# The experts' loop of a hybrid encoder block: weight loads in longer runs, low parts and loads on other queues, earlier gathers

## The chip, the core and the metric

The kernel runs on one core of a Trainium2 chip. Its time is the device time of one execution in microseconds (us), and less is better. The engines are named as the profile names them: PE is TensorE's matrix unit and PEld its weight load, DVE is VectorE, ACT is ScalarE, POOL is GpSimd, SP is the sync engine, which here only issues DMAs. Each engine works through its own queue in order and waits for semaphores.

## The reference, cut

The block is a bidirectional mixer (a long convolution and a state space scan) followed by a mixture of experts, each with a residual and a layer norm. 1024 tokens of 1024 values go through it, in float32. The change lies in the mixture of experts: a router picks 8 of 64 experts for each token, and each expert is a gated two-layer network with 256 hidden values.

```python
def routed_experts(h2d, idx, w, w_gate, w_up, w_down):
    ...
    def step(acc, blk):
        tok, wt, e = blk
        xb = h_pad[tok]
        hb = jax.nn.silu(xb @ w_gate[e]) * (xb @ w_up[e])
        yb = (hb @ w_down[e]) * wt[:, None]
        return acc.at[tok].add(yb.astype(acc.dtype)), None
...
def moe_sublayer(h, router_w, router_bias, exp_w_gate, exp_w_up, exp_w_down,
                 sh_w_gate, sh_w_up, sh_w_down):
    ...
    idx, w = route(h2d, router_w, router_bias)
    routed = routed_experts(h2d, idx, w, exp_w_gate, exp_w_up, exp_w_down)
    shared = (jax.nn.silu(h2d @ sh_w_gate) * (h2d @ sh_w_up)) @ sh_w_down
    return (routed + shared).reshape(bsz, seq, d)
...
    h = layer_norm(DN_ALPHA * h + ffn, ln2_g[i], ln2_b[i])
```

## The kernel before, in words

The stages before the experts (projections, scan, convolutions, merge, router) take the first 2350 us or so and are not touched, except for one view in the shared expert (`sh_gu`). The experts' loop is in `moe`.

The router sorts the experts by load, so that the place of an expert in that order (its rank r) has a fixed capacity `caps[r]`: 16 experts of 192 rows, 16 of 160, 16 of 128 and 16 of 112. `order` takes a large and a small one in turn. Each expert is cut into blocks of at most 128 rows; three blocks (128, then 64 or 32, then 128 or 112 rows) make two experts, and there are 96 blocks in all. Index tables (`slot_tables`) tell which token each row of a block holds. They are made for eight experts at a time, during the eight experts before, one step of the generator `tj` per block; each step compares on DVE (line 2071, tile oh) and multiplies on PE (line 2079).

Every float32 matmul is done as products of a high and a low part (`mm3`: three matmuls, `both_mm`: two with the parts of the rows side by side, for blocks of 32 or 64 rows). An expert's weights come as three tiles of 1 MB, numbered p: two with four k-slices each of gate and up, one with down. For each tile there are three steps. `w_load` issues the DMA into a raw buffer eraw (line 1599). `w_hi` rounds on ACT to ehi (line 1611). `w_lo` subtracts to elo (line 1618): on DVE for the two gate and up tiles, on POOL for the down tile. When the low part is done the raw buffer is free, and `lo_load` at once issues the load of tile p + 6 into it.

The gate and up slices of one k lie next to each other in a raw tile (256 values of gate, 256 of up), so that one matmul takes 512 columns of both. The source of a DMA has 4 KB in a row for each partition, but each 1 KB of it goes to another place.

For each block b the loop does, in this order: `gather(b + 3)` (POOL, an indirect DMA from h_d into a tile xg, line 1625); the casts `w_hi` of two tiles; the gate and up matmuls, with `lo_load` of a tile and `hidden(b - 1)` between k = 3 and k = 4; the activation; `xpose(b + 2)`, which transposes gathered rows on PE (line 1640) and splits them into xgh and xgl; `lo_load` of the second tile; a table step; `down(b - 1)`, the down matmuls, whose result yo (two buffers) an indirect DMA of POOL adds into scr_acc in HBM (line 1661). These scatter-adds read and write the same tensor, so each waits until the one before it has landed. `hidden` transposes the activated rows and splits them into hb (line 74). For the small blocks the activation goes through a tile lows, whose last step is the product of line 1877 on DVE.

The rows xg have three buffers: one in the pool of raw tiles, for every third block, and two elsewhere. `gather(b + 3)` writes the buffer that `xpose(b)` has read.

All five engines run in the order in which the code issues the instructions (`manual_schedule`). The loads of gate and up are on SP's queue, the down load, the gathers, the scatters and the low part of down on POOL's.

Of the kernel before, what the change touches and what calls it, by code (L numbers as in the profile page):

```python
# [9 lines left out]
F32 = mybir.dt.float32  # L10
# [5 lines left out]
ALU = mybir.AluOpType  # L16
# [3 lines left out]
P = 128  # L20
ET = mybir.EngineType
MANUAL = {ET.SP, ET.PE, ET.Activation, ET.DVE, ET.Pool}
D = 1024
# [18 lines left out]
class Kern:  # L42
# [107 lines left out]
    def w_load(self, pool, c0, n=P):  # L150
        raw = pool.tile([P, KT, P], F32, name="wraw", bufs=2)
        self.nc.sync.dma_start(raw[:, :, :n], self.a["w_in"][0, :, c0:c0 + n].rearrange("(k p) c -> p k c", p=P))
        return raw
# [1056 lines left out]
    def merge(self):  # L1210
        nc, a, tc = self.nc, self.a, self.tc
# [105 lines left out]
        with ExitStack() as cx:  # L1317
            cx.callback(p1.release)
            pool = cx.enter_context(tc.tile_pool(name="mh", bufs=1, reuse_waits="tile"))
# [16 lines left out]
            for p in range(3):  # L1336
# [4 lines left out]
                for o in range(2 if p == 0 else 0, 8):  # L1341
                    i = p * 8 + o
                    ps = [self.bank(), self.bank()]
# [12 lines left out]
                    elif p == 1:  # L1356
                        for h in range(2):
                            v = sr[o][:, h * 512:(h + 1) * 512]
                            TT(v, v, ps[h], ALU.add)
                        STT(sr[o], gt.pop((p, o)), 1.0, sr[o], ALU.add, ALU.mult)  # L1360
                    else:
                        g = gt.pop((p, o))
                        for h in range(2):
                            v = g[:, h * 512:(h + 1) * 512]
                            STT(v, v, 1.0, ps[h], ALU.add, ALU.mult)
                        TT(g, g, sr[o], ALU.add)
                        for h in range(2):
                            v = g[:, h * 512:(h + 1) * 512]
# [85 lines left out]
                    sh[q] = [[v[:, h * 512:(h + 1) * 512] for v in hl] for h in range(2)]  # L1454

            def sh_gu(t):
                gu = [sh[k // 2][k % 2] for k in range(8)]
                for k, ps in enumerate(self.swi_gu(lhs(t), gu, P)):
                    if k < 7:
                        yield  # L1460
                yield self.swi_act(pool, ps, P, ld()[:, 0:256])
# [100 lines left out]
    def moe(self):  # L1562
# [3 lines left out]
        with ExitStack() as cx:  # L1566
# [17 lines left out]
            def w_load(p):  # L1584
                if p >= 192:
                    return
                i, q = divmod(p, 3)
                eng = nc.gpsimd if q == 2 else nc.sync
                if q != 1:
                    weng[0] = eng.value_load(self.eid[0:1, order[i]:order[i] + 1], min_val=0, max_val=63)  # L1590
                g, u, d = [a[n][0][bass.ds(weng[0], 1)].rearrange("o (p j) c -> (o p) j c", p=P)
                           for n in ("exp_w_gate", "exp_w_up", "exp_w_down")]
                parts = ((g[:, 0:4], u[:, 0:4]), (g[:, 4:8], u[:, 4:8]), (d,))[q]
                wraw[p] = rps[i % 2].tile([P, 2048], F32, name="eraw", bufs=3)
                v = wraw[p].rearrange("p (k c) -> p k c", k=parts[0].shape[1])
                c0 = 0
                for src in parts:
                    n = src.shape[2]
                    eng.dma_start(v[:, :, c0:c0 + n], src)
                    c0 += n  # L1600

            def w_hi(p, c=slice(0, 2048)):
                if p >= 192:
                    return
                if p not in whl:
                    i, q = divmod(p, 3)
                    hi, lo = whl[p] = [wps[i % 2].tile([P, 2048], F32R, name=f"e{c}", bufs=3) for c in ("hi", "lo")]
                    k = 2 if q == 2 else 4
                    wsplit.setdefault(i, []).extend(zip(*[[v.rearrange("p (k c) -> p k c", k=k)[:, j] for j in range(k)]
                                                          for v in (hi, lo)]))  # L1610
                nc.scalar.copy(whl[p][0][:, c], wraw[p][:, c])  # L1611

            def w_lo(p, c=slice(0, 2048)):
                if p >= 192:
                    return
                eng = nc.gpsimd if p % 3 == 2 else nc.vector
                hi, lo = whl[p]
                eng.tensor_tensor(lo[:, c], wraw[p][:, c], hi[:, c].bitcast(F32), ALU.subtract)  # L1618

            def gather(b):  # L1620
                if b >= len(blocks):
                    return
                i, r, s, o, n = blocks[b]
                t = rps[0].tile([P, D], F32, name="xg") if b % 3 == 0 else pool.tile([P, D], F32, name="xg", bufs=2)
                nc.gpsimd.indirect_dma_start(out=t[:n, :], out_offset=None, in_=self.h_d,  # L1625
                                             in_offset=bass.IndirectOffsetOnAxis(ap=tabs[r][s][0], axis=0))
                gath[b] = t

            def xpose(b):
                if b >= len(blocks):  # L1630
                    return
                i, r, s, o, n = blocks[b]
                t = gath.pop(b)
                xh = pool.tile([P, 8, P], F32R, name="xgh", bufs=2)
                xl = xh[:, :, n:2 * n] if n in (32, 64) else pool.tile([P, 8, P], F32R, name="xgl", bufs=2)
                for h in range(2):
                    ps = self.bank("B")
                    for j in range(4):
                        k = h * 4 + j
                        nc.tensor.transpose(ps[:, j * P:j * P + n], free(t[:n, k:k + 1], [[8, P]]), self.ident[:n, :n])  # L1640
                    src = ps.rearrange("p (j t) -> p j t", t=P)[:, :, :n]
                    self.split(src, xh[:, h * 4:h * 4 + 4, :n], xl[:, h * 4:h * 4 + 4, :n])
                xts[b] = xh[:, :, :2 * n] if n in (32, 64) else [(xh[:, k, :n], xl[:, k, :n]) for k in range(8)]

            def hidden(b):
                if b >= 0:
                    n = blocks[b][4]
                    hbs[b] = (self.both_h if n in (32, 64) else self.swi_h)(pool, sgs.pop(b), n)

            def down(b):  # L1650
                if b < 0 or b >= len(blocks):
                    return
                i, r, s, o, n = blocks[b]
                y = pool.tile([P, D], F32, name="yo", bufs=2)
                wd = [[(h[:, q * 512:(q + 1) * 512], l[:, q * 512:(q + 1) * 512]) for q in range(2)] for h, l in wsplit[i][8:10]]
                if n in (32, 64):
                    self.both_down(hbs.pop(b), wd, y, n)
                else:
                    for q, ps in enumerate(p for p in self.swi_down(pool, hbs.pop(b), wd, n) if p is not None):
                        nc.scalar.activation(y[:n, q * 512:(q + 1) * 512], ps[:n, :], AF.Copy, scale=tabs[r][s][2])  # L1660
                nc.gpsimd.indirect_dma_start(  # L1661
                    out=self.acc_d, out_offset=bass.IndirectOffsetOnAxis(ap=tabs[r][s][1], axis=0),
                    in_=y[:n, :], in_offset=None, compute_op=ALU.add, oob_is_err=True, bounds_check=L + P - 1)
# [37 lines left out]
            cw.enter_context(tc.manual_schedule(engines=MANUAL))  # L1701
            gather(1)
            gather(2)
            for p in range(3, 6):
                w_load(p)
            xpose(0)
            for p in range(2):
                for c in [slice(c * 512, c * 512 + 512) for c in range(4)]:
                    w_hi(p, c)
                    w_lo(p, c)  # L1710
                w_load(p + 6)
            xpose(1)
            tj = iter(())

            def lo_load(p):
                w_lo(p)
                w_load(p + 6)
            for b, (i, r, s, o, n) in enumerate(blocks):
                if s == 0:
                    if i % 8 == 0 and i < 56:  # L1720
                        for _ in tj:
                            pass
                        tj = table_jobs(i // 8 + 2)
                gather(b + 3)
                w_hi(2 * b + 2)
                w_hi(2 * b + 3)
                x, gu = xts.pop(b), wsplit[i][0:8]
                for k, ps in enumerate((self.both_gu if n in (32, 64) else self.swi_gu)(x, gu, n)):
                    if k == 3:
                        lo_load(2 * b + 2)  # L1730
                        hidden(b - 1)
                if n in (32, 64):
                    sgs[b] = self.both_act(pool, ps, tabs[r][s][2], n)
                else:
                    sgs[b] = self.swi_act(pool, ps, n)
                xpose(b + 2)
                lo_load(2 * b + 3)
                next(tj, None)
                down(b - 1)
# [82 lines left out]

    def swi_gu(self, lhs, gu, n):
        ps = self.bank()
        for k in range(8):
            self.mm3(ps[:n, :], lhs[k][0], lhs[k][1], gu[k][0], gu[k][1], k == 0, k == 7)
            yield ps

    def swi_act(self, pool, ps, n, sg=None):
# [34 lines left out]

    def both_gu(self, x, gu, n):
        ps = self.bank()
        for k in range(8):
            self.both_mm(ps, x[:, k], n, gu[k][0], gu[k][1], k == 0, k == 7)
            yield ps

    def both_act(self, pool, ps, w, n):
# [499 lines left out]
```

## Time and profile before

| | |
|---|---|
| median of 3 runs | 3530.07 us (3528.78 to 3532.55) |
| the profiled execution | 3534.84 us, span from first to last instruction 3533.2 us |
| busy share of the span | PE 90%, DVE 73%, POOL 47%, ACT 40% |
| mean granted clock of TensorE | 0.943 of full |
| mean DMA rate | 152 GB/s |
| gate and up loads | 256 DMAs of 512 KB on SP's queue |
| down loads | 64 DMAs of 1024 KB on POOL's queue |
| gathers, scatters | 96 and 96 indirect DMAs on POOL's queue |

The profile lists one execution. An instruction's row has its start from the beginning of the span, its length, its engine and line, the tiles out<-in, and in brackets how long the engine was idle before it and what ended that. Shares of busy time are means over stages with different limits, so a stage has to be read by itself. A DMA queue's share is the time that its packets took, over 16 DMA engines.

### The profile page before, as it was taken

To read this page: it belongs to the slowest core of one execution; us is meant where nothing else is said; L and a number is where in the kernel's file an instruction comes from. 1 tells how busy PE (TensorE), PEld (TensorE's weight loads), DVE (VectorE), ACT (ScalarE), POOL (GpSimd) and SP (SyncE) were. 2 spreads that over 40 slices of the span, in tenths; PEclk is the share of its full clock that TensorE was granted. 3 is DMA by queue.
4 is the path that set the end of the run, shared out by engine and by line. 5 is a ranking of instruction groups with operands and counts; after the bars stand their busy time and mean duration, and the time that the engine had idled before them with its cause. 6 is when DMAs were issued, how large, how long until landed. Compare 5 with 4: busy or idle time off the path is not lost. (4 is left out here: it accounts for less than half of the span.)

```text
span 3533.2 us, 42386 instructions
## 1 busy us (share of the span) xinstructions
PE 3188.0 (90%) x14923; PEld 2506.6 (71%) x14923; DVE 2590.6 (73%) x3551; ACT 1406.7 (40%) x2206; POOL 1676.7 (47%) x1480
## 2 busy tenths in 40 slices
PE   8989998989998998899999999997889888888893
PEld 6767776777777777567888888875666666666662
DVE  6787887888787878557994344657778787677786
ACT  3334333343334232322223212415656555565663
POOL 2545454555454546441110320215667667777774
PEclk9999899999999999899999999988999999899996
DMA  4323232322322322744325445327999899888894
GB/s 131 78 72 87 67 96 75 85 73 79 91 78 75 89 72 91 215 147 151 106 90 173 126 155 158 107 85 242 271 271 270 259 259 262 250 249 249 250 283 128
DMA packets 439908, 538.22 MB, mean 152 GB/s; under 512 B 24361, under 2 KB 373325, under 8 KB 430989
## 3 DMA queue, kind: packets, MB, share of 16 engines
q1 hardware_dynamic: 404717, 379.23, 36.6%
q0 software_dynamic: 33824, 152.06, 15.0%
q10 hardware_dynamic: 1152, 4.19, 0.3%
q8 instruction: 119, 1.95, 0.2%
q14 instruction: 96, 0.79, 0.1%
HBM read 430.29 MB, written 105.12 MB: 152 GB/s over the span
## 5 line engine op out<-in xcount | busy, mean ns | idle before, releaser
L170 PE MATMUL bankA<-xth,whi 128*128 128x512 f32 (+1 forms) x1424 | 470.1, 412 | 0.5 <-ACT whi L73 0.3
L170 PE MATMUL bankA<-xtl,whi 128*128 128x512 f32 (+1 forms) x1424 | 452.6, 400 | 0.0
L170 PE MATMUL bankA<-xth,wlo 128*128 128x512 f32 (+1 forms) x1424 | 449.4, 397 | 1.5 <-POOL wlo L74 1.5
L1618 DVE TENSOR_TENSOR elo<-eraw,ehi 128x2048 fp32r<-128x2048 f32 (+1 forms) x134 | 393.7, 2945 | 18.9 <-ACT ehi L1611 13.1
L1661 POOL DMA_INDIRECT scr_acc<-yo,sidx x96 | 231.1, 2407 | 275.9 <-DMA scr_acc<-yo,sidx 147.1
L1611 ACT CAST ehi<-eraw 128x2048 fp32r<-128x2048 f32 (+1 forms) x198 | 356.3, 1852 | 3.3 <-DMA eraw<-in_exp_w_gate_dram 3.3
L74 POOL TENSOR_TENSOR wlo<-wraw,whi 128x1024 fp32r<-128x1024 f32 (+1 forms) x89 | 225.4, 2532 | 278.1 <-ACT whi L73 278.1
L170 PEld LDWEIGHTS bankA<-xtl,whi 128*128 128x128 f32 (+1 forms) x1424 | 274.5, 193 | 64.1 <-DVE xtl L74 0.4
L170 PEld LDWEIGHTS bankA<-xth,wlo 128*128 128x128 f32 (+1 forms) x1424 | 272.2, 191 | 64.5 <-POOL wlo L74 2.0
L170 PEld LDWEIGHTS bankA<-xth,whi 128*128 128x128 f32 (+1 forms) x1424 | 268.2, 195 | 58.3 <-issue 5.4
L1618 POOL TENSOR_TENSOR elo<-eraw,ehi 128x2048 fp32r<-128x2048 f32 x64 | 298.1, 4658 | 15.8 <-ACT ehi L1611 14.7
L399 POOL TENSOR_SCALAR Wm<-cbm,dt 128x128 f32<-128x128 f32 x256 | 129.9, 507 | 348.2 <-DVE cbm L373 348.2
L1625 POOL DMA_INDIRECT xg<-scr_h,gidx x96 | 182.3, 1899 | 63.4 <-issue 24.3
L79 PE MATMUL bankA<-elo,xgh 128*128 128x512 f32 (+1 forms) x512 | 203.6, 398 | 8.6 <-DVE elo L1618 8.6
L78 PE MATMUL bankA<-ehi,xgh 128*128 128x512 f32 (+1 forms) x512 | 210.1, 410 | 0.0
L80 PE MATMUL bankA<-ehi,xgl 128*128 128x512 f32 (+1 forms) x512 | 203.3, 397 | 0.0
L1640 PE MATMUL bankB<-ident,xg 128*128 128x128 f32 (+3 forms) x768 | 113.4, 295 | 94.0 <-DMA xg<-scr_h,gidx 92.5
L1640 PEld LDWEIGHTS bankB<-ident,xg 128*128 128x128 f32 (+3 forms) x768 | 101.5, 198 | 122.9 <-issue 107.5
L74 DVE TENSOR_TENSOR xgl<-bankB,xgh 128x512 fp32r<-128x512 f32 (+1 forms) x128 | 81.3, 664 | 107.7 <-ACT xgh L73 106.0
L80 PE MATMUL bankA<-ehi,hb 128*128 128x512 f32 (+1 forms) x256 | 121.3, 474 | 27.0 <-DVE hb L74 26.9
L1877 DVE SCALAR_TENSOR_TENSOR lows<-lows,wt 64x256 f32<-64x256 f32 (+1 forms) x32 | 132.5, 4140 | 15.5 <-ACT lows L1876 15.5
L393 DVE SCALAR_TENSOR_TENSOR Em<-bcs,Acs,Em 128x128 f32<-128x128 f32 x256 | 140.9, 609 | 2.3
(551 smaller groups left out, 7672.7 us busy)
## 6 DMA issues: line engine op xcount, KB each, us to landing
eraw<-in_exp_w_gate_dram SPq DMA_DIRECT2D x128, 512.0 KB, 5.9
eraw<-in_exp_w_down_dram POOLq DMA_DIRECT2D x64, 1024.0 KB, 6.0
eraw<-in_exp_w_up_dram SPq DMA_DIRECT2D x128, 512.0 KB
wraw<-in_w_in_dram SPq DMA_DIRECT2D x88, 512.0 KB, 4.1
bcs<-scr_at SPq DMA_DIRECT2D x128, 256.0 KB, 5.6
scr_K<-kout SPq DMA_DIRECT2D x32, 512.0 KB, 2.8
Kt<-scr_K SPq DMA_DIRECT2D x32, 512.0 KB, 3.5
scr_gate<-accf SPq DMA_DIRECT2D x16, 512.0 KB, 4.2
```

Source lines behind the costliest of these rows:

```text
L74: (lo_eng or nc.vector).tensor_tensor(lo, src, hi.bitcast(F32), ALU.subtract)
L78: mm(out, sh, mh, start=first, stop=False)
L79: mm(out, sh, ml, start=False, stop=False)
L80: mm(out, sl, mh, start=False, stop=last)
L170: mm(ps[h], wt[:, k, :n], x[:, h * 512:(h + 1) * 512], start=(k == 0 and f == 1), stop=(k == KT - 1 and l == 1))
L393: STT(E[:, h], bcs[:, 1, h], self.A[:, c, 32 + j:33 + j], E[:, h], ALU.subtract, ALU.min)
L1611: nc.scalar.copy(whl[p][0][:, c], wraw[p][:, c])
L1618: eng.tensor_tensor(lo[:, c], wraw[p][:, c], hi[:, c].bitcast(F32), ALU.subtract)
L1625: nc.gpsimd.indirect_dma_start(out=t[:n, :], out_offset=None, in_=self.h_d, in_offset=bass.IndirectOffsetOnAxis(ap=tabs[r][s][0], axis=0))
L1640: nc.tensor.transpose(ps[:, j * P:j * P + n], free(t[:n, k:k + 1], [[8, P]]), self.ident[:n, :n])
L1661: nc.gpsimd.indirect_dma_start(out=self.acc_d, out_offset=bass.IndirectOffsetOnAxis(ap=tabs[r][s][1], axis=0), in_=y[:n, :], in_offset=Non ...
L1877: nc.vector.scalar_tensor_tensor(t[:, 0:256], t[:, 0:256], w, t[:, 256:512], ALU.mult, ALU.mult)
```

## The change

The raw tiles of gate and up hold first the four slices of gate, then those of up, so that each DMA writes 4 KB in a row per partition; the matmuls take their 512 columns as two pieces of 256. Down loads are issued by SP and the low part of down is made on DVE, so POOL keeps only gathers and scatters. Raw tiles rotate over five buffers instead of six (three in one pool, two in the other), so a tile's successor is p + 5; the result tile yo has four buffers instead of two. `gather(b + 5)` behind `xpose(b + 2)` takes the place of `gather(b + 3)` at the block's start, and two more gathers stand ahead of the loop. `hidden(b - 1)` comes before the `lo_load` of k = 3. In the blocks of every eighth expert a second table step stands at k = 5. The line numbers move by up to four.

```diff
@@ sh_gu
-                gu = [sh[k // 2][k % 2] for k in range(8)]
+                gu = [[v.rearrange("p (s c) -> p s c", s=2) for v in sh[k // 2][k % 2]] for k in range(8)]
@@ w_load
-                eng = nc.gpsimd if q == 2 else nc.sync
-                if q != 1:
+                eng = nc.sync
+                if q == 0:
                     weng[0] = eng.value_load(self.eid[0:1, order[i]:order[i] + 1], min_val=0, max_val=63)
...
-                wraw[p] = rps[i % 2].tile([P, 2048], F32, name="eraw", bufs=3)
-                v = wraw[p].rearrange("p (k c) -> p k c", k=parts[0].shape[1])
-                c0 = 0
-                for src in parts:
-                    n = src.shape[2]
-                    eng.dma_start(v[:, :, c0:c0 + n], src)
-                    c0 += n
+                wraw[p] = rps[p % 5 // 3].tile([P, 2048], F32, name="eraw", bufs=3 - p % 5 // 3)
+                v = wraw[p].rearrange("p (s k c) -> p s k c", s=len(parts), k=parts[0].shape[1])
+                for n, src in enumerate(parts):
+                    eng.dma_start(v[:, n], src)
@@ w_hi
-                    k = 2 if q == 2 else 4
-                    wsplit.setdefault(i, []).extend(zip(*[[v.rearrange("p (k c) -> p k c", k=k)[:, j] for j in range(k)]
+                    k, n = (2, 1) if q == 2 else (4, 2)
+                    wsplit.setdefault(i, []).extend(zip(*[[v.rearrange("p (s k c) -> p k s c", s=n, k=k)[:, j] for j in range(k)]
@@ w_lo
-                eng = nc.gpsimd if p % 3 == 2 else nc.vector
                 hi, lo = whl[p]
-                eng.tensor_tensor(lo[:, c], wraw[p][:, c], hi[:, c].bitcast(F32), ALU.subtract)
+                nc.vector.tensor_tensor(lo[:, c], wraw[p][:, c], hi[:, c].bitcast(F32), ALU.subtract)
@@ down
-                y = pool.tile([P, D], F32, name="yo", bufs=2)
+                y = pool.tile([P, D], F32, name="yo", bufs=4)
@@ ahead of the loop
-            for p in range(3, 6):
+            for p in range(3, 5):
                 w_load(p)
             xpose(0)
+            gather(3)
...
-                w_load(p + 6)
+                w_load(p + 5)
             xpose(1)
+            gather(4)
             tj = iter(())

             def lo_load(p):
                 w_lo(p)
-                w_load(p + 6)
+                w_load(p + 5)
@@ the loop over blocks
-                gather(b + 3)
                 w_hi(2 * b + 2)
                 w_hi(2 * b + 3)
...
                     if k == 3:
+                        hidden(b - 1)
                         lo_load(2 * b + 2)
-                        hidden(b - 1)
+                    if k == 5 and i % 8 == 0:
+                        next(tj, None)
...
                 xpose(b + 2)
+                gather(b + 5)
                 lo_load(2 * b + 3)
@@ swi_gu, and both_gu alike
+        p3 = ps[:n, :].rearrange("p (s c) -> p s c", s=2)
         for k in range(8):
-            self.mm3(ps[:n, :], lhs[k][0], lhs[k][1], gu[k][0], gu[k][1], k == 0, k == 7)
+            self.mm3(p3, lhs[k][0], lhs[k][1], gu[k][0], gu[k][1], k == 0, k == 7)
```

On POOL, about halfway through the loop, three blocks (two experts) of the kernel before stand in its queue like this; TENSOR_LOAD and ISA read the expert's number for the down load.

```order
L1661 DMA scr_acc<-yo,sidx_22035 1152x1024
L1625 DMA xg<-scr_h,gidx_23292 128x1024
L1618 TENSOR_TENSOR elo<-eraw,ehi 128x2048
L1590 TENSOR_LOAD eid
L1590 ISA x2
L1599 ISA
L1599 DMA eraw<-in_exp_w_down_dram 128x2048
L1661 DMA scr_acc<-yo,sidx_22022 1152x1024
L1625 DMA xg<-scr_h,gidx_23305 32x1024
L1618 TENSOR_TENSOR elo<-eraw,ehi 128x2048
```

The same engine and place in the changed kernel:

```order
L1621 DMA xg<-scr_h,gidx_22836 32x1024
L1657 DMA scr_acc<-yo,sidx_21638 1152x1024
L1621 DMA xg<-scr_h,gidx_22823 112x1024
L1657 DMA scr_acc<-yo,sidx_21625 1152x1024
L1621 DMA xg<-scr_h,gidx_22823 128x1024
```

What moved: the low part and the down load have left this queue, and a gather now stands two blocks further ahead of the scatter beside it.

On DVE, a small block and the large one behind it, at about the same place, before:

```order
L74 TENSOR_TENSOR hb<-bankC,hb 128x256
L1875 TENSOR_TENSOR lows<-lows,bankA 64x512
L1877 SCALAR_TENSOR_TENSOR lows<-lows,wt_22037 64x256
L74 TENSOR_TENSOR xgl<-bankB,xgh 128x512 x2
L1618 TENSOR_TENSOR elo<-eraw,ehi 128x2048
L74 TENSOR_TENSOR hb<-bankC,hb 128x2x64
L1834 TENSOR_TENSOR sg<-sg,bankA 128x256
L74 TENSOR_TENSOR xgh<-bankB,xgh 128x4x32 x2
L1618 TENSOR_TENSOR elo<-eraw,ehi 128x2048
```

and now:

```order
L74 TENSOR_TENSOR hb<-bankC,hb 128x256
L1614 TENSOR_TENSOR elo<-eraw,ehi 128x2048
L1877 TENSOR_TENSOR lows<-lows,bankA 64x512
L1879 SCALAR_TENSOR_TENSOR lows<-lows,wt_21640 64x256
L74 TENSOR_TENSOR xgl<-bankB,xgh 128x512 x2
L1614 TENSOR_TENSOR elo<-eraw,ehi 128x2048
L74 TENSOR_TENSOR hb<-bankC,hb 128x2x64
L1614 TENSOR_TENSOR elo<-eraw,ehi 128x2048
L1835 TENSOR_TENSOR sg<-sg,bankA 128x256
L74 TENSOR_TENSOR xgh<-bankB,xgh 128x4x32 x2
L1614 TENSOR_TENSOR elo<-eraw,ehi 128x2048
```

What moved: each block now has two low parts, the first of them behind hb and ahead of the block's own activation.

On SP, one expert's loads before, and then now:

```order
L1599 DMA eraw<-in_exp_w_gate_dram 128x4x256
L1599 ISA
L1599 DMA eraw<-in_exp_w_up_dram 128x4x256
L1599 ISA
L1599 DMA eraw<-in_exp_w_gate_dram 128x4x256
L1599 ISA
L1599 DMA eraw<-in_exp_w_up_dram 128x4x256
```

```order
L1597 DMA eraw<-in_exp_w_gate_dram 128x1024
L1597 ISA
L1597 DMA eraw<-in_exp_w_up_dram 128x1024
L1597 ISA
L1597 DMA eraw<-in_exp_w_gate_dram 128x1024
L1597 ISA
L1597 DMA eraw<-in_exp_w_up_dram 128x1024
L1597 ISA
L1597 DMA eraw<-in_exp_w_down_dram 128x2048
```

What moved: the down load stands behind the others of its expert, and what a partition receives of a gate or up DMA is one piece of 1024 values instead of four of 256.

## Rows read from the trace of the kernel before

**Rows 1.** Windows: stretch, its length, busy time by engine, PEclk, DMA share, GB/s.

```profile
2450.00:3450.00 1000.00, 878.38 (x4397) 659.90 (x4395) 773.84 (x763) 597.30 (x747) 701.96 (x299) 0.93 0.90 261
3400.00:3450.00 50.00, 45.95 (x204) 33.14 (x204) 39.30 (x46) 32.63 (x42) 31.52 (x16) 0.97 0.97 289
```

**Rows 2.** Waits, 2450 to 3450 us: total us, times, longest us.

```profile
POOL scr_acc L1661 <- DMA scr_acc<-yo,sidx: 147.1, 32, 8.0
...
PE bankB L1640 <- DMA xg<-scr_h,gidx: 91.2, 35, 5.5
...
PE bankA L80 <- DVE hb L74: 20.4, 18, 1.9
```

**Rows 3.** Timeline of POOL: start us, length us, instruction, idle before it.

```profile
2907.61 2.47 POOL L1625 DMA_INDIRECT xg<-scr_h,gidx  x1 [0.30 <-issue]
2916.50 1.46 POOL L1661 DMA_INDIRECT scr_acc<-yo,sidx  x1 [6.41 <-DMA scr_acc<-yo,sidx]
2918.26 0.99 POOL L1625 DMA_INDIRECT xg<-scr_h,gidx  x1 [0.30 <-PE bankB L1640]
2919.27 4.60 POOL L1618 TENSOR_TENSOR elo<-eraw,ehi 128x2048 fp32r<-128x2048 f32 x1
...
2925.06 2.44 POOL L1661 DMA_INDIRECT scr_acc<-yo,sidx  x1 [0.30 <-issue]
...
2937.71 1.62 POOL L1661 DMA_INDIRECT scr_acc<-yo,sidx  x1 [3.12 <-DMA scr_acc<-yo,sidx]
...
2947.60 1.45 POOL L1661 DMA_INDIRECT scr_acc<-yo,sidx  x1 [4.96 <-DMA scr_acc<-yo,sidx]
```

**Rows 4.** Timeline of PE across a wait for a gather.

```profile
2913.38 0.40 PE L79 MATMUL bankA<-elo,xgh 128*128 128x512 f32 x1
2913.61 0.40 PE L80 MATMUL bankA<-ehi,xgl 128*128 128x512 f32 x1
2917.55 1.13 PE L1640 MATMUL bankB<-ident,xg 128*128 128x128 f32 x8 [3.54 <-DMA xg<-scr_h,gidx]
...
2919.56 0.63 PE L78 MATMUL bankA<-ehi,hb 128*128 128x512 f32 x1
2919.98 0.63 PE L79 MATMUL bankA<-elo,hb 128*128 128x512 f32 x1
```

**Rows 5.** Page part 6, a weight load: KB, median us from issue to landing.

```profile
eraw<-in_exp_w_gate_dram SPq DMA_DIRECT2D x128, 512.0 KB, 5.9
```

**Rows 6.** Groups by line, 2450 to 3450 us.

```profile
L1618 DVE TENSOR_TENSOR elo<-eraw,ehi 128x2048 fp32r<-128x2048 f32 x120 | 363.5, 3032 | 10.1 <-ACT ehi L1611 10.0
...
L1611 ACT CAST ehi<-eraw 128x2048 fp32r<-128x2048 f32 x180 | 333.5, 1904 | 0.0
...
L1877 DVE SCALAR_TENSOR_TENSOR lows<-lows,wt 64x256 f32<-64x256 f32 (+1 forms) x30 | 128.7, 4290 | 14.5 <-ACT lows L1876 14.5
```

**Rows 7.** Line 1618 on DVE, 2450 to 3450 us: duration ns min/median/max.

```profile
L1618 DVE TENSOR_TENSOR elo<-eraw,ehi x120: 2269/2280/7342, 2448.4 to 3441.9; 128x2048 fp32r<-128x2048 f32 x120
```

**Rows 8.** Line 1877, whole run: duration ns min/median/max.

```profile
L1877 DVE SCALAR_TENSOR_TENSOR lows<-lows,wt x32: 476/4309/4391, 2427.2 to 3461.7; 64x256 f32<-64x256 f32 x16, 32x256 f32<-32x256 f32 x16
```

**Rows 9.** Timeline of DVE beside the gather at 2907.61.

```profile
2906.93 2.27 DVE L1618 TENSOR_TENSOR elo<-eraw,ehi 128x2048 fp32r<-128x2048 f32 x1
```

**Rows 10.** DMA queue, 2450 to 3450 us: packets, MB, share of 16 engines.

```profile
q1 hardware_dynamic: 125056, 124.80, 43.5%
```

**Rows 11.** The same columns, 2355 to 2372 us.

```profile
q1 hardware_dynamic: 2112, 2.10, 39.6%
...
q10 hardware_dynamic: 280, 1.05, 15.1%
```

**Rows 12.** Tile scr_acc, 2450 to 3450 us: the scatters and their landing.

```profile
L1661 POOL DMA_INDIRECT scr_acc<-yo,sidx x90: 1359/2003/5654, 2452.8 to 3449.9; - x90
...
DMA to landing us min/median/max: 3.5/10.2/14.1
```

**Rows 13.** Tile xg, 2450 to 3450 us: landing of the gathers.

```profile
DMA to landing us min/median/max: 4.2/9.1/11.6
```

More of the change, by code (lines that the diff above doesn't have):

```diff
@@ L1653, in down @@
                 i, r, s, o, n = blocks[b]
-                y = pool.tile([P, D], F32, name="yo", bufs=2)
-                wd = [[(h[:, q * 512:(q + 1) * 512], l[:, q * 512:(q + 1) * 512]) for q in range(2)] for h, l in wsplit[i][8:10]]
+                y = pool.tile([P, D], F32, name="yo", bufs=4)
+                wd = [[(h[:, 0, q * 512:(q + 1) * 512], l[:, 0, q * 512:(q + 1) * 512]) for q in range(2)] for h, l in wsplit[i][8:10]]
                 if n in (32, 64):
@@ L1866, in both_gu @@
         ps = self.bank()
+        p3 = ps.rearrange("p (s c) -> p s c", s=2)
         for k in range(8):
-            self.both_mm(ps, x[:, k], n, gu[k][0], gu[k][1], k == 0, k == 7)
+            self.both_mm(p3, x[:, k], n, gu[k][0], gu[k][1], k == 0, k == 7)
             yield ps
```

## The prediction

> **What bounds the kernel now.** I read the windows first. The change touches the experts' loop and, outside it, only a view of the shared expert's weights, so I leave the other 2530 us as they are. In 2450 to 3450 us, which is most of the loop, TensorE works 878.38 of 1000 us at a granted clock of 0.93, while DMA is at 0.90, VectorE at 774 us and POOL at 702 us [rows 1].
>
> TensorE idles 121.6 us of that stretch. The waits say for what: 91.2 us for gathered rows (xg), 20.4 us for the low part of the hidden rows (hb), which leaves 10.0 us for everything else [rows 2]. The idle time costs again: matmuls that start 0.23 us apart before a wait start 0.42 us apart behind it, the lower level of 1.2 GHz instead of 2.4 [rows 4]. In the last 50 us of the stretch, where TensorE idles least, the clock is 0.97 [rows 1]. At 0.93 the whole lacks 7% of its clock, 70 us, or 0.58 us for each idle us. So TensorE's own work at the upper level is 878.4 - 70 = 808 us.
>
> Why is a gather late? POOL takes its queue in order, and each scatter-add into scr_acc waits for the one before it to land: 147.1 us of idle time [rows 2]. In the timeline the scatter at 2937.71 waits 3.12 us for its predecessor, and the next at 2947.60 waits 4.96 us; between 2916.50 and 2925.06 POOL is instead held by a gather, a 4.60 us low part and a load issue [rows 3]. These three steps, 8.56, 12.65 and 9.89 us, make 31.1 us, and 90 scatters in 1000 us are 33.3 us for three [rows 12]. So the bound is POOL's chain of scatters, with the low parts in it. Gathers stand in the same queue and land 9.1 us after their issue in the median, 11.6 at most [rows 13]. The one at 2907.61 [rows 3] is what TensorE waits 3.54 us for until 2917.55 [rows 4]: it left 10 us ahead of its use, one block, not the two blocks for which the code asks.
>
> **Early gathers.** gather(b+5) stands right behind xpose(b+2), which frees its buffer, and is used by xpose(b+5) three blocks on. A block is 11.1 us now and would be some 9.7 us, so the lead is about 29 us against a landing of at most 11.6 us [rows 13]. Even one scatter of 12.65 us ahead of it in the queue leaves slack. I take the 91.2 us as gone (bounds: 30 left, if POOL lags by two scatters; 0).
>
> **Low parts on VectorE.** 180 casts less 120 low parts on VectorE in the stretch leave 60 for POOL [rows 6]. They now cost VectorE 60 times 2.28 us, the median of line 1618 [rows 7], = 137 us. What VectorE gets back: its low parts average 3.03 us [rows 6] with a longest of 7.34 us [rows 7], the long ones beside a POOL low part; 120 x (3.03 - 2.28) = 90 us. Line 1877, a 256-column product, lasts 4.29 us on average [rows 6], and 0.48 us once [rows 8]: 30 x 3.81 = 114 us. So VectorE goes from 774 to 774 + 137 - 90 - 114 = 707 us. The upper bound for it is that nothing comes back: 60 x 3.03 = 182 us more, 956 us. I take 707, since the 2.28 us is the median and the short case of line 1877 has the same shape. The other way round, a gather lasts 0.99 us at 2918.26 and 2.47 us at 2907.61 [rows 3], where a low part that began at 2906.93 runs on beside it [rows 9]; so more low parts on VectorE can slow POOL's issues, which is rival 3. The Trainium skill ("SBUF — State Buffer", section "Who interferes with whom") takes a VectorE tensor_tensor not to hold up the building of descriptors; by it rival 3 would have no price at all, but the trace differs by the 1.48 us between those two gathers.
>
> **The order on VectorE.** hb now stands ahead of the low part at k = 3, so it no longer waits behind 2.28 us of it. Of 20.4 us I keep 10 (bounds 0 and 20.4).
>
> **4 KB runs and the down loads on SP.** In the stretch q1 moves 124.80 MB of 1 KB pieces in a share of 43.5%, 435 us or 3.49 us per MB [rows 10]. From 2355 to 2372 us two kinds of rows run side by side: 1 KB pieces take 39.6% of 17 us for 2.10 MB, 3.21 us per MB, and the nearly 4 KB pieces of q10 take 15.1% for 1.05 MB, 2.44 us per MB [rows 11]. That is 24% less; on 435 us some 104 us (bounds 0 and 131, from 3.49 to 2.44). I take 90, since q10 stores and these are loads: DMA falls from 900 to 810 us. It ends no wait by itself: the casts never idle for a weight [rows 6]. The 1 MB down loads leave the queue of the scatters, in which one is issued between the low part of 2919.27 and the scatter at 2925.06, right ahead of it [rows 3].
>
> **The scatters.** They land after 3.5 to 14.1 us, 10.2 in the median [rows 12]. Without POOL's low parts the 8.56 us step becomes that of a small scatter, near the 3.5 us; the two large ones cost 12.65 and 9.89 us at most as today. So the chain is 26 us for three, 780 us for the stretch, and at most today's 31.1 us, 933 us.
>
> **What I cost at nothing.** Five raw buffers instead of six: the load of tile p + 5 is issued some 1.6 blocks, 15 us, ahead of its cast, and lands in 5.9 us [rows 5]; if it took longer than 15 us, each us late would cost one per block, 96 us in all. The extra table step at k = 5 in the two blocks of every eighth expert moves a step of VectorE forward; VectorE has 226 idle us in the stretch [rows 1], and if that cover is gone, its place in the queue is all that changes, for the number of steps is the same. SP issues five loads per expert where it issued four and POOL one; SP does nothing else in the loop. Four result buffers end no wait of today, and cover scatters that lag. The views of the two weight halves leave the matmuls at 512 columns.
>
> **The sum.** In the stretch: 808 us of TensorE work; idle time 0 + 10 + 10.0 = 20 us; clock lost with it 20 x 0.58 = 12 us: 840 us. Beside it stand DMA with 810, the scatter chain with 780 and VectorE with 707 us. Four queues so close don't overlap fully; I add 35 us for that, half of what would take it to 910 (the chain at 30.3 us for three), a choice. 875 us, so 125 us less for 90 blocks and 133 for all 96. The profiled execution took 3534.8 us around its 3533.2 us span; that gives 3402, and the runs' median lies 4.8 us lower: **3400 us** rounded.
>
> **The rivals.**
> 1. The chain of scatters keeps its pace. For it: each scatter still waits for the last one's landing, and the two large ones alone cost 22.5 us. Against: the down load no longer stands ahead of them. At 31.1 us for three the stretch takes 933 us, 67 less, 71 for 96 blocks: 3459 us.
> 2. The longer runs save no DMA time beside the gathers and scatters. DMA stays at 900 us; at the share of 0.97 which the last 50 us of the stretch reach [rows 1], 928 us, 72 less, 77 in all: 3453 us. The Trainium skill ("DMA: Bandwidth & Descriptors", section "Why small descriptors are slow (HBM only)") gives a fixed cost of about 3 cycles beside 32 for 1 KB, so an estimate of 6% off 435 us, 26 us, which would give 901 us at that share and 3424 us. The rows side by side show four times that, under a lighter load.
> 3. Slower: VectorE's low parts, 180 now, hold POOL's descriptor building. The longest scatter instruction is 5.65 us, the median 2.00 [rows 12]. If both large scatters of each three get 3.2 us longer, three take 31.1 + 6.4 = 37.5 us, 1125 us in the stretch: 133 us more, 3663 us. It decides from 33.3 us for three, 2.2 us above today's chain. Against it: VectorE's total falls.
> 4. The change does not do what it says: POOL reaches the gathers as late as before, since they stand behind scatters that wait. TensorE keeps its 91.2 us: about 3530 us.
>
> **How the numbers follow.** Forecast 0.58 (own range 3345 to 3440: 827 us in the stretch, 12 us of idle time and no coupling, at the one end; 916 us, 76 of coupling, at the other), rival 1 0.18, rival 2 0.12, rival 3 0.07, rival 4 0.05. The range 3345 to 3500 holds the first three less their tails. Rivals 1 and 2 are faster too: faster by over 0.2% (7 us, about what a measurement of this kernel can tell from no change) 0.88, within it 0.05, slower 0.07.
>
> **What the profile of the changed kernel would show.** Right: TensorE's wait for xg under 15 us, PEclk above 0.97, the product of line 1877 near 0.5 us, the low parts at 2.28 us without long ones, q1 under 2.9 us per MB, 90 blocks in about 875 us. Rival 1: POOL idle for landing scatters, ACT or TensorE waiting behind it. Rival 2: casts idle for eraw with DMA at 0.95. Rival 3: scatters of over 4 us in the median. What would make me wrong most: TensorE waiting for low parts, because VectorE in its order is late though not full.

## The result and the profile after

The changed kernel takes 3410.52 us (median of 4 runs, 3402.69 to 3413.53), the kernel before 3529.43 us on the same chip: a ratio of 0.9666, 95% interval 0.9637 to 0.9694, some 119 us less. The forecast was 3400 us. The profiled execution took 3412.94 us around a span of 3411.2 us. I read it over 2450 to 3330 us: its 880 us hold 4370 matmul records, where the 1000 us of [rows 1] held 4397.

Windows of the changed kernel (columns as in [rows 1]): that stretch, the loop's last 15 us, and the end.

```profile
2450.00:3330.00 880.00, 836.74 (x4370) 636.32 (x4368) 694.50 (x821) 591.94 (x748) 313.90 (x175) 0.97 0.96 294
...
3330.00:3345.00 15.00, 13.41 (x58) 9.36 (x58) 8.19 (x10) 5.46 (x12) 3.10 (x3) 1.00 0.42 66
3345.00:3411.00 66.00, 1.02 (x5) 0.45 (x3) 36.78 (x59) 12.66 (x19) 21.11 (x11) 0.53 0.44 145
```

TensorE now works 95% of the stretch at 0.97 of its clock. Its idle 43 us have another cause than before, as the waits show (engine, line and tile, what ended the wait; us, times, longest):

```profile
POOL scr_acc L1657 <- DMA scr_acc<-yo,sidx: 170.9, 29, 10.4
...
PE bankD L2081 <- DVE oh L2073: 34.5, 12, 3.9
...
PE bankB L1636 <- DMA xg<-scr_h,gidx: 8.3, 6, 1.9
```

Against [rows 2], the wait for xg fell from 91.2 to 8.3 us, and that for hb from 20.4 to 0.4. What has grown is the wait for oh, the compare of a table step: 34.5 us. In the 1000 us of before it was short:

```profile
PE bankD L2079 <- DVE oh L2071: 5.9, 7, 1.6
```

POOL still waits for scatters to land.

The groups by line that answer to [rows 6]:

```profile
L1614 DVE TENSOR_TENSOR elo<-eraw,ehi 128x2048 fp32r<-128x2048 f32 x180 | 410.8, 2282 | 0.0
L1608 ACT CAST ehi<-eraw 128x2048 fp32r<-128x2048 f32 x180 | 333.8, 1909 | 0.0
...
L1879 DVE SCALAR_TENSOR_TENSOR lows<-lows,wt 64x256 f32<-64x256 f32 (+1 forms) x30 | 14.3, 475 | 14.5 <-ACT lows L1878 14.5
```

All low parts last 2.28 us, and the product that averaged 4.29 us now takes 0.48 us. The casts never idle for weights.

Where does the wait for oh come from? VectorE around one of them, and behind it TensorE:

```profile
2770.64 2.28 DVE L1614 TENSOR_TENSOR elo<-eraw,ehi 128x2048 fp32r<-128x2048 f32 x1
2772.84 1.75 DVE L2073 TENSOR_TENSOR oh<-iota,posm 128x1536 bf16<-128x1536 int16 x1
```

```profile
2769.75 1.04 PE L1636 MATMUL bankB<-ident,xg 128*128 128x128 f32 x8
2774.64 0.87 PE L2081 MATMUL bankD<-aux,oh 128*128 128x6 bf16 x16 [3.85 <-DVE oh L2073]
2775.45 0.80 PE L78 MATMUL bankA<-ehi,hb 128*128 128x512 f32 x1
2776.04 0.63 PE L79 MATMUL bankA<-elo,hb 128*128 128x512 f32 x1
2776.46 0.63 PE L80 MATMUL bankA<-ehi,hb 128*128 128x512 f32 x1
```

The compare of the extra step at k = 5 stands behind hb and a low part on VectorE, and is ready at 2774.6; the step at the block's end multiplies with it, and TensorE, past its transposes at 2770.8, waits 3.85 us. Behind the wait matmuls start 0.42 us apart, the lower level of 1.2 GHz again, as in [rows 4].

POOL's timeline over three blocks, which answers to [rows 3]:

```profile
2951.74 1.72 POOL L1657 DMA_INDIRECT scr_acc<-yo,sidx  x1 [6.31 <-DMA scr_acc<-yo,sidx]
2953.77 0.96 POOL L1621 DMA_INDIRECT xg<-scr_h,gidx  x1 [0.31 <-issue]
2960.19 1.50 POOL L1657 DMA_INDIRECT scr_acc<-yo,sidx  x1 [5.47 <-ACT xgh L73]
...
2967.42 1.96 POOL L1657 DMA_INDIRECT scr_acc<-yo,sidx  x1 [2.94 <-DMA scr_acc<-yo,sidx]
...
2979.90 1.36 POOL L1657 DMA_INDIRECT scr_acc<-yo,sidx  x1 [8.30 <-DMA scr_acc<-yo,sidx]
```

A scatter, a gather, then idle time that ends, before three of these four scatters, with the landing of the one before: 28.2 us for three blocks here, and 88 scatters in 880 us are 30.0 us for three. At the end the chain of waits shows that scatters lag behind TensorE, whose last matmul starts at 3345.62:

```profile
3344.72 6.97 DMA scr_acc<-yo,sidx
...
3352.47 3.46 DMA scr_acc<-yo,sidx
...
3356.69 5.98 DMA scr_acc<-yo,sidx
```

From TensorE's last matmul to the end of the span it is 65.6 us, against 56.6 us before (3476.65 to 3533.2): 9 us are given back there.

### The profile page after: what moved, and what is told of

It reads as the page before. It is cut to its first block, busy times and chain, and to the rows that moved or that the text cites. A ratio compares the mean times of both kernels' runs of the same rounds, so it can differ in the third digit from the quotient of the medians.

```text
span 3411.2 us, 42203 instructions
## 1 busy us (share of the span) xinstructions
PE 3143.2 (92%) x14922; PEld 2480.5 (73%) x14923; DVE 2509.4 (74%) x3615; ACT 1400.9 (41%) x2206; POOL 1267.0 (37%) x1352
## 5 line engine op out<-in xcount | busy, mean ns | idle before, releaser
L1614 DVE TENSOR_TENSOR elo<-eraw,ehi 128x2048 fp32r<-128x2048 f32 (+1 forms) x198 | 438.5, 2217 | 2.4 <-DMA scr_acc<-sr 2.4
L1657 POOL DMA_INDIRECT scr_acc<-yo,sidx x96 | 187.2, 1950 | 554.2 <-DMA scr_acc<-yo,sidx 185.3
L399 POOL TENSOR_SCALAR Wm<-cbm,dt 128x128 f32<-128x128 f32 x256 | 130.7, 511 | 346.9 <-DVE cbm L373 346.9
L1621 POOL DMA_INDIRECT xg<-scr_h,gidx x96 | 150.8, 1571 | 139.2 <-DVE idf L2050 54.1
L74 DVE TENSOR_TENSOR hb<-bankC,hb 128x256 fp32r<-128x256 f32 (+3 forms) x96 | 34.8, 363 | 170.5 <-ACT hb L73 170.3
L430 DVE TENSOR_TENSOR yt<-yt,off 128x256 f32<-128x256 f32 x112 | 136.0, 1214 | 3.9
L394 ACT ACTIVATE Em<-Em 128x512 f32<-128x512 f32 x64 | 40.4, 631 | 225.3 <-DVE Em L393 225.3
L400 POOL TENSOR_SCALAR Wm<-cbm,dt 128x128 f32<-128x128 f32 x256 | 127.7, 499 | 0.0
L1656 ACT ACTIVATE yo<-bankA,wt 128x512 f32<-128x512 f32 (+1 forms) x128 | 85.6, 693 | 101.0 <-PE bankA L80 100.9
L1035 PE MATMUL bankA<-sdf,Fm 128*128 128x256 f32 x512 | 124.3, 386 | 1.6 <-DVE U L1052 1.6
```

Source lines behind the costliest of these rows:

```text
L74: (lo_eng or nc.vector).tensor_tensor(lo, src, hi.bitcast(F32), ALU.subtract)
L399: nc.gpsimd.tensor_scalar(W[:, h], cbm[:, 0], self.dt[:, c, j:j + 1], 0.0, ALU.mult, ALU.add)
L430: TT(y, y, off[:, d], ALU.add)
L1614: nc.vector.tensor_tensor(lo[:, c], wraw[p][:, c], hi[:, c].bitcast(F32), ALU.subtract)
L1657: nc.gpsimd.indirect_dma_start(out=self.acc_d, out_offset=bass.IndirectOffsetOnAxis(ap=tabs[r][s][1], axis=0), in_=y[:n, :], in_offset=Non ...
```

## The experiments

My theory after this reading: the early gathers made the gain, and TensorE is now bound by its own work, the wait for oh and a chain of scatters that just keeps pace. Rivals: DMA, at 0.96, is the bound and the longer runs made the gain; or what counts is what was taken off POOL's queue. All kernels start from the changed one. The kernel before, timed again beside each group of runs, took 3528 to 3535 us, so small differences are better read from the ratios. "Idle" is TensorE's in 2450 to 3330 us.

| kernel | median us | ratio to before, 95% interval | idle us |
|---|---|---|---|
| changed | 3410.5 | 0.9666 (0.9637 to 0.9694) | 43.3 |
| step at k = 2 | 3395.1 | 0.9616 (0.9596 to 0.9636) | 39.7 |
| 1 KB pieces | 3405.1 | 0.9645 (0.9625 to 0.9665) | 36.2 |
| late gathers | 3517.5 | 0.9967 (0.9952 to 0.9982) | 93.4 |
| low part of down on POOL | 3526.9 | 0.9996 (0.9984 to 1.0009) | 116.0 |
| two accumulators (half left out) | 3407.5 | 0.9640 (0.9611 to 0.9669) | 36.9 |
| the same, step at k = 2 | 3365.7 | 0.9520 (0.9493 to 0.9548) | ends earlier |
| two result buffers | 3440.2 | 0.9738 (0.9708 to 0.9768) | 57.3 |
| down loads on POOL | 3440.7 | 0.9723 (0.9685 to 0.9761) | 64.6 |
| two accumulators, summed, k = 2 | 3364.3 | 0.9529 (0.9503 to 0.9554) | ends earlier |
| the same, 1 KB pieces | 3366.1 | 0.9539 (0.9512 to 0.9565) | ends earlier |
| low part ahead of hb | 3400.7 | 0.9618 (0.9577 to 0.9658) | 42.3 |
| two accumulators (half left out), low part on POOL | 3528.1 | 0.9982 (0.9966 to 0.9997) | 95.5 |

**1 KB pieces.**

```diff
-v = wraw[p].rearrange("p (s k c) -> p s k c", ...)
+v = wraw[p].rearrange("p (k s c) -> p s k c", ...)
... (the views of the two weight halves alike)
```

> The changed kernel with the 1 KB pieces of before in the raw tiles of gate and up (gate and up of a k side by side), everything else as changed. Theory: a MB in 1 KB pieces takes 3.49 us of DMA, as before, against 2.93 us now (62.1% of 880 us for 186.81 MB). On the 125 MB of gate and up that is 70 us more, so the stretch's 845 us of DMA become 915; at a share of 0.97 the stretch takes 943 us, 63 more: about 3475 us, with casts or TensorE waiting for weights. Rival (the forecast's second): the piece length saves no DMA time; then within 10 us of 3411 us.

The rival was right: 3405 us, no slower. Its queue q1, and above it that of the changed kernel (packets, MB, share), both over 2450 to 3330 us:

```profile
q1 hardware_dynamic: 42959, 186.81, 62.1%
```

```profile
q1 hardware_dynamic: 134754, 188.77, 65.8%
```

880 x 0.621 / 186.81 is 2.93 us per MB, and 880 x 0.658 / 188.77 is 3.07: q1 as a whole costs 4.9% more, some 27 us. A third of its MB are down loads, which the edit leaves alone; laid on gate and up alone it is some 7%, an estimate, not the 24% that I took from [rows 11]. The 3.49 of [rows 10] can't be set beside 2.93, for q1 held no down loads there. In the run below with down loads on POOL, gate and up alone take 3.12 us per MB in their 4 KB pieces (880 x 0.427 / 120.51):

```profile
q1 hardware_dynamic: 33251, 120.51, 42.7%
```

DMA went from 0.96 to 0.99 with the 1 KB pieces, and no wait followed. The Trainium skill ("DMA: Bandwidth & Descriptors", section "Why small descriptors are slow (HBM only)") came closer than my rows, with its fixed cost per packet, from which the forecast's estimate was 6%.

**Late gathers.**

```diff
+                gather(b + 3)
                 w_hi(2 * b + 2)
...
                 xpose(b + 2)
-                gather(b + 5)
... (the two gathers ahead of the loop go too)
```

> The changed kernel with gather(b + 3) at the block's start again, and no gathers ahead of the loop; everything else as changed. Theory: the early gathers are what takes TensorE's waits for xg away; two blocks ahead, behind a scatter that waits, most of the 91 us come back, and part of the clock: 3475 to 3530 us. Rival: with low parts and loads off POOL's queue the gathers leave in time even so; then 3410 to 3430 us, and the wait for xg stays below 25 us.

3517.5 us, as the theory had it: 107 us of the gain go back. Its waits:

```profile
PE bankB L1636 <- DMA xg<-scr_h,gidx: 70.1, 25, 4.8
...
PE bankD L2079 <- DVE oh L2071: 23.4, 6, 4.0
```

**Low part of down on POOL.**

```diff
-nc.vector.tensor_tensor(lo[:, c], ...)
+(nc.gpsimd if p % 3 == 2 else nc.vector).tensor_tensor(lo[:, c], ...)
```

> The changed kernel with the low part of the down tile on POOL again; down loads stay on SP, gathers early. Theory: TensorE is the bound and the early gathers cover a late POOL, so the low parts in the chain of scatters cost little: 3411 to 3435 us. Rival (the forecast's first): the chain of scatters with the low part in it sets the pace at 31.1 us for three blocks again, and the run takes about 3460 us, POOL idle for landing scatters and TensorE or ACT waiting behind a full yo. In both, line 1879 lasts over 4 us again and low parts on VectorE average about 3 us.

Neither: 3526.9 us, all of the gain gone although the gathers stay early. TensorE waits here for the low part itself, and for oh longer than the 34.5 us of the changed kernel:

```profile
PE bankD L2081 <- DVE oh L2073: 51.8, 14, 7.8
...
PE bankA L79 <- POOL elo L1614: 46.3, 17, 6.5
```

Is it the place in the scatters' queue? The last run of this list takes that reason away: with two accumulators no scatter of its stretch waits for a landing, where the changed kernel has 170.9 us.

> Two accumulators (half of the results left out, the step at k = 5) with the low part of the down tile on POOL. On POOL's queue with one accumulator it took the whole gain back (3527 us). Theory: it did so because it stands behind scatters that wait for their predecessor's landing, and TensorE waits for the low part; with two chains POOL hardly waits, and the run takes 3407 to 3440 us with TensorE's wait for POOL's elo under 15 us. Rival: it did so because VectorE and POOL slow each other (VectorE's low part 3.01 instead of 2.28 us, POOL's 4.86 us); then 3480 us or more even so.

The rival was right: 3528.1 us. TensorE's wait for POOL's elo is gone, and these two stand among its waits:

```profile
PE bankC L1889 <- DVE lows L1881: 52.1, 20, 2.7
...
PE bankD L2083 <- DVE oh L2075: 43.3, 12, 3.9
```

They make 95.4 of its 95.5 idle us. With two accumulators and all low parts on VectorE oh was 36.5 us already and lows did not stand among the waits, so what the low part on POOL adds is the 52.1 us for lows and 7 us of oh, with the clock that goes with them (0.98 there, 0.93 here). POOL and VectorE side by side in this run:

```profile
2952.37 5.04 POOL L1616 TENSOR_TENSOR elo<-eraw,ehi 128x2048 fp32r<-128x2048 f32 x1
...
2973.53 5.20 POOL L1616 TENSOR_TENSOR elo<-eraw,ehi 128x2048 fp32r<-128x2048 f32 x1
```

```profile
2953.80 0.42 DVE L74 TENSOR_TENSOR hb<-bankC,hb 128x256 fp32r<-128x256 f32 x1 [2.70 <-ACT hb L73]
2954.14 4.90 DVE L2075 TENSOR_TENSOR oh<-iota,posm 128x1536 bf16<-128x1536 int16 x1
...
2972.54 1.75 DVE L2075 TENSOR_TENSOR oh<-iota,posm 128x1536 bf16<-128x1536 int16 x1
...
2975.36 3.64 DVE L1881 SCALAR_TENSOR_TENSOR lows<-lows,wt 32x256 f32<-32x256 f32 x1 [0.48 <-ACT lows L1880]
```

The same compare takes 1.75 us when it begins before POOL's low part, and 4.90 us when it begins beside one; line 1881 (1879 in the changed kernel, 0.48 us there) ends with POOL's low part, at 2979.0 beside 2978.7. The compare of 4.90 us ends at 2959.04, 1.63 us behind its low part, nearly its own 1.75: it looks as if it stood still until POOL was done. The instruction for hb at 2953.80, one of whose inputs is in PSUM (bankC), keeps its 0.42 us beside the same low part. So a low part on POOL costs by stretching VectorE's work on two tiles of SBUF next to it, and TensorE waits for that, here for lows above all. The Trainium skill ("SBUF — State Buffer", section "Who interferes with whom") says that a VectorE instruction with both inputs in SBUF contends with a GpSimd instruction that reads SBUF; the rows agree, 1.75 against 4.90 us.

**Step at k = 2.**

```diff
-                    if k == 5 and i % 8 == 0:
+                    if k == 2 and i % 8 == 0:
```

> The changed kernel with its extra table step at k = 2 instead of k = 5, so that the compare (oh) stands ahead of hb and the low part on VectorE and not behind them. Theory: TensorE bounds the loop of the changed kernel, and of the 43 us that it idles in 2450 to 3330 us, 34.5 us are waits for oh. They go, and with them some 0.58 us of clock for each: 20 us. Expected 3360 to 3380 us, no wait of TensorE for oh above 5 us in all. Rival: DMA, at 0.96 of its time in the stretch, bounds it; then the idle time only moves to another wait, and the run ends within 10 us of the changed kernel's 3411 us.

3395 us, 15 us less where I expected 31 to 51. The profiled execution, the longest of its four at 3409 us, shows the wait for oh gone, and others come:

```profile
POOL scr_acc L1657 <- DMA scr_acc<-yo,sidx: 209.3, 33, 10.2
...
PE bankB L1636 <- DMA xg<-scr_h,gidx: 34.6, 22, 5.6
...
PE bankD L2081 <- DVE oh L2073: 4.4, 4, 1.7
```

POOL waits longer for scatters, and gathers behind them are late again: 34.6 us.

**Two accumulators.** The chain can be split without leaving a wait out: blocks add in turn into two tensors.

```diff
-out=self.acc_d, ...
+out=(self.acc_d, self.acc2_d)[b % 2], ...
... (acc2_d starts as a copy of acc_d and is left out of the end)
```

> The changed kernel with the blocks' results scattered in turn into two accumulators, so that a scatter waits for the landing of the one before the last; the second accumulator starts as a copy of the first and is left out of the end (half of the blocks' results are dropped, and 4 MB more are written before the loop). Theory: in the changed kernel the chain of scatters runs at the loop's pace (a scatter, a gather, then POOL idle until the landing: 28 to 30 us for three blocks), so it lags at the end, where five scatters follow each other from 3326.9 to 3362.7 us behind TensorE's last work near 3346 us. With two chains POOL's idle time for landing scatters (170.9 us) falls under 40 us, the tail shortens by 8 to 15 us, and TensorE keeps its 34.5 us for oh: 3390 to 3403 us. Rival: TensorE and DMA alone set the end, and the chain is only idle time of an engine that is not the bound: 3405 to 3415 us.

The rival was right, 3407.5 us: alone, the split gives nothing that these runs can tell, and TensorE keeps 36.5 us for oh. With the step at k = 2:

> The same two accumulators, and the extra table step at k = 2. With the step at k = 2 alone the waits for oh went (34.5 to 4.4 us) but waits for xg came (8.3 to 34.6 us). Theory: those came because a gather stands behind a scatter that waits for its predecessor; with two chains both waits stay under 10 us in 2450 to 3330 us, the granted clock reaches 0.99, TensorE's 812 us of work set the pace, and the run takes 3345 to 3375 us. Rival: DMA, at 0.96 there, is the limit; then gathers and loads land later instead, and the run takes 3385 to 3400 us with TensorE idle for xg or for weights.

The theory held: 3365.7 us. Moving the step gave 15 us, splitting the chain 3 us, both 45 us (18, 9 and 52 by the ratios to before). Each took one of two waits away that stood behind each other.

**The two, with the whole result.** This kernel computes all of the reference.

```diff
+                nc.sync.dma_start(xs[i], self.acc2_d[...])
+                nc.gpsimd.dma_start(xs[i], self.acc_d[...], accum_op=ALU.add)
-                nc.sync.dma_start(xs[i], self.acc_d[...])
... (acc2_d starts at zero)
```

> Two accumulators and the step at k = 2, now with the whole result: the second accumulator starts at zero (written ahead of the merge) and the last stage loads it and adds the first to it by an accumulating DMA on POOL's queue. Theory: the loop is that of the run with half of the results left out (3366 us), and the end pays one more DMA behind the first tile's load, 4 to 12 us: 3370 to 3380 us. Rival: the eight accumulating loads, whose descriptors POOL builds one after the other, set the pace of the last stage; then 3385 us or more, and little is left of the gain over the step at k = 2 alone (3395 us).

3364.3 us, better than both kernels, and below the range of the theory: the sum costs nothing that can be told from the run before. Its window, and that of the same kernel with 1 KB pieces (next expectation):

```profile
2450.00:3300.00 850.00, 833.55 (x4450) 634.43 (x4448) 704.62 (x832) 598.89 (x763) 422.51 (x180) 1.00 0.98 307
```

```profile
2450.00:3300.00 850.00, 834.17 (x4453) 634.81 (x4451) 704.37 (x832) 599.46 (x763) 420.48 (x180) 1.00 1.01 308
```

> The kernel with two accumulators, their sum and the step at k = 2, with 1 KB pieces in the raw tiles. With 1 KB pieces the changed kernel was no slower (3405 us) though q1 took 3.07 instead of 2.93 us per MB and DMA stood at 0.99. Theory: there TensorE's other waits hid it; in the faster kernel DMA is at 0.98 already, and 5% more on q1's 64% are 3 points that no longer fit: 10 to 25 us slower than the same kernel with 4 KB pieces. Rival: the share is no limit, since packets that wait beside each other count in it; then within 6 us of it.

3366.1 us: the rival was right. The clock is 1.00 and TensorE's last matmul starts at 3294, so it idles some 10 us. 1 KB pieces cost nothing that can be told even here, with a DMA share of 1.01.

**Two result buffers, and down loads on POOL.**

```diff
-y = pool.tile([P, D], F32, name="yo", bufs=4)
+y = pool.tile([P, D], F32, name="yo", bufs=2)
```

> The changed kernel with two result buffers instead of four. The forecast put the four buffers at nothing for the waits of before. Theory: the chain of scatters now lags TensorE, by three scatters at the end, so with two buffers ACT waits for a free yo, TensorE for a free bank: 3425 to 3460 us, with ACT yo waiting for scr_acc. Rival: lagging scatters are a matter of the last blocks alone; then 3405 to 3418 us.

```diff
-eng = nc.sync
-if q == 0:
+eng = nc.gpsimd if q == 2 else nc.sync
+if q != 1:
```

> The changed kernel with the down loads issued on POOL's queue again, the low part of down staying on VectorE. Theory: unlike the low part, a load issue holds POOL for less than 1 us, but it stands behind scatters that wait up to 10 us for their predecessor, and with five raw buffers its lead is some 15 us against a landing near 7 us; so the casts of down wait little: 3411 to 3430 us. Rival: whatever stands in the scatters' queue is late for TensorE, as the low part was (3527 us): over 3460 us, casts idle for the down load.

3440.2 and 3440.7 us: 30 us more each by the medians, 25 and 20 by the ratios to before. The first is as the theory had it, the second 10 us above its range. In the first, ACT waits for a result buffer that a scatter still reads; in the second, the casts wait for a down load that left late. In both TensorE then waits for the rows that ACT made:

```profile
ACT yo L1656 <- DMA scr_acc<-yo,sidx: 36.6, 9, 6.8
...
PE bankA L78 <- ACT hb L73: 20.1, 6, 5.1
```

```profile
ACT ehi L1608 <- DMA eraw<-in_exp_w_down_dram: 28.0, 5, 6.3
PE bankA L78 <- ACT hb L73: 27.7, 5, 6.2
```

**Low part ahead of hb.**

```diff
-                        hidden(b - 1)
                         lo_load(2 * b + 2)
+                        hidden(b - 1)
```

> The changed kernel with the low part ahead of hb at k = 3 again. The forecast kept 10 of the 20.4 us for hb. Theory: hb is now 2.3 us later on VectorE in every block, and TensorE reads it only at the block's end, so the waits for hb come back in the short blocks alone: 3405 to 3422 us, wait for hb under 15 us. Rival: with the loop at 10 us a block the whole 20 us come back with their clock; 3430 to 3445 us.

3400.7 us (3386.8 to 3413.2), an interval that overlaps the changed kernel's: no gain of the order is to be seen, and perhaps a small loss; the median is 4 us below the range of the theory. The wait for hb is 0.4 us here too. That for oh shrinks to 6.8, and xg takes its place with 34.3 us.

## Why the prediction was right, and where its steps were not

The sum, for the work of [rows 1]: 880 x 4397 / 4370 = 885 us, against a forecast of 875.

- **TensorE's work at the upper clock**: 808 us forecast. The summed kernel shows it at a clock of 1.00: 833.55 x 4397 / 4450 = 824 us. My division by the mean clock was 16 us short.
- **Idle time**: 20 us forecast, 43.5 measured (43.3 scaled). xg kept 8.3 us for a forecast of 0, hb 0.4 for 10. One step failed: what I costed at nothing, the table step at k = 5, took the wait for oh from 5.9 us, within the 10.0 for everything else, to 34.5. I had argued from VectorE's 226 idle us [rows 1] that only its place in the queue changes, and its place was the price.
- **Clock**: 12 us forecast; 885 - 824 - 44 leaves 17.
- **The order on VectorE**: the wait for hb went, but not for the reason given. With the low part ahead of hb again it is 0.4 us all the same; what took it away is not shown.
- **Coupling**: the 35 us were a choice. No general coupling shows; 24 us of idle time and 5 of clock beyond the forecast, with the 16 above, fill the place. That the sum came within 10 us of the measured stretch is in part luck.
- **Early gathers**: right, and needed: undone, 107 us go back.
- **Low parts on VectorE**: VectorE's total was right (694.5 us, 699 scaled, for 707), and line 1877's fall too. The reason was wrong. I had put the value into the chain of scatters, 26 us for three instead of 31.1. The chain fell to 28 to 30 us, and the run with two chains shows that the low part on POOL costs all of the gain without it, through the stretched work of VectorE: 52.1 us of waits for lows. I had booked that as 90 and 114 us of VectorE's time off the path.
- **4 KB runs**: this step failed. I forecast 24% of what gate and up take, and 90 us of DMA; it is some 7% of them by the estimate above, or 27 us, and 0.96 x 880 is still 845 us. The rows side by side [rows 11] set stores on an almost empty queue against loads. Rival 2 was nearly right about the saving and wrong about its price: a DMA share of 0.99 or 1.01 bounded nothing.
- **Four result buffers and down loads on SP**: costed at nothing from the waits of before. There was nothing to gain there, but in the loop as changed each is worth 20 to 30 us.
- **Five raw buffers**: right, the casts idle 0.0 us.
- **Rivals 1, 3 and 4**: the chain moved some, though it lags by 9 us at the end; the scatters' median fell from 2.00 to 1.60 us, so 60 more low parts on VectorE did not slow the issues of scatters in the median; the gathers came in time, but for 8.3 us.

Gain by part can't be added: late gathers alone, or the low part on POOL alone, take nearly all of it back. A sixth raw buffer was not tried in the changed kernel. What late gathers and a low part on POOL cost in the kernel before, one at a time, was not run.

## What to carry to other kernels

A wait hides those behind it: before costing an edit at nothing because no wait of today asks for it, ask who comes last once the big wait is gone, and undo that edit in the changed kernel. When an edit gives less than its wait was long, look for a second wait that ends just before the first; here two edits worth 15 and 3 us alone, the 3 within the scatter of the runs, gave 45 together. Work moved off a slow engine can pay on its neighbour, so compare the durations of the same instruction with and without it.

## What was not expected of the hardware

- A DMA share of 1.01 with no wait for a weight, and 308 GB/s: a share above 1 can only come of packets counted side by side, so 1 is no ceiling.
- Loads in 1 KB pieces cost some 7% more DMA time than in 4 KB pieces here (an estimate from 4.9% on all of q1), and no time of the kernel that can be told.
- Whichever VectorE instruction with two SBUF inputs stands beside POOL's low part takes the loss: with two accumulators line 1881 has a median of 4.68 us; with one, where the low part falls elsewhere, the same line (1879 there) has a median of 0.51 us, against the 4 us that I expected, and compares of 1.2 us take 5.6.
